# RWKV-7 recurrence in a hybrid decoder step: keys and values on the other head's rows, the values' part taken out of the chunk recurrence, 3 instead of 5 quanta of the next products per late tick

## Chip, cores and metric

One of the eight NeuronCores of a Trainium2 chip runs the kernel. The metric is the device time of one execution in microseconds; the median of several runs counts.

## What is computed

A four-layer decoder trunk (HGRN2, RWKV-7, Mamba-2, HGRN2, each followed by a SwiGLU FFN) is run in fp32 for one prompt of 512 tokens and for 8 sequences of 4 new tokens, with the same weights. Activations lie as 8 tiles of 128 features x 544 tokens (512 prompt, 32 sample). The change concerns the RWKV-7 layer over the prompt. Its recurrence, for each of 16 heads of 64:

```python
def step(s, inp):
    r_t, w_t, k_t, v_t, kk_t, a_t = inp
    sa = jnp.einsum('bhvk,bhk->bhv', s, -kk_t)
    s = (s * w_t[:, :, None, :] + sa[..., None] * (kk_t * a_t)[:, :, None, :]
         + v_t[..., None] * k_t[:, :, None, :])
    return s, jnp.einsum('bhvk,bhk->bhv', s, r_t)
```

After it come a norm by head, a bonus r.k.v, a gate, the output projection and the FFN.

## The kernel before

The prompt's 512 tokens are cut in chunks of 64. A `_Pair` (L998) is two feature tiles, so four heads, over half of the prompt, which is four chunks; there are eight pairs, 0 to 3 for the first half of the tokens and 4 to 7 for the second. The two heads of a tile lie on the row halves 0-63 and 64-127 (`ROWS`, called `e` in the code; `OTH` is the same two, exchanged). A pair is worked off by three generators:

- `front` (L1057) makes for each of its two tiles (`i`) and each chunk (`q`): the transposed values VT, the scores of b and k (BK) against a and r (AR) in one product of 128 columns (masked into SW[0], SB for b and SW[1], SK for k), the transposed b and k (TK), W = SW[1] times VT, the transposed a (AT), and the bonus with `heads_sum` (L973). `keys` (L1015) loads and prepares the operands; its last step writes bn (L1054), of which there are two buffers and which `front` later stores to DRAM (L1121).
- `inv` (L1126) inverts the 64x64 triangular matrices with 32x32 products and ends with U and XA.
- `back` (L1191) walks the four chunks in turn. Per chunk: U += XA z (`psc`, L1206 and L1207), then the state's increment from VT and U (`pp`, L1212), the new state zz (L1215 or L1217), and the output in `po`, which sums VT SK, z R and U SB (L1224). z is scaled on GpSimd first (zd, L1204). At its end O is copied out of PSUM (L1229), the norm by head follows and the gated output is written.

`_rwkv_main` (L874) interleaves them. Stage `s` runs `back` of pair s-2, `inv` of pair s-1 and `front` of pair s, each one step per tick, for twelve ticks. Each tick ends with some quanta of large products: in stages 0 to 5 the r and v projections, in stages 6 to 9 PART = 5 quanta of `end`, the output projection and FFN of the first 256 tokens. A quantum is two of the eight 128-row steps of a product, so six matmuls of 256 columns (`Part.mm`, L265). In this loop TensorE's instructions stand in program order (`ordered`, L73); those of the other engines are placed by the planner. `end` has 298 quanta, of which 240 run in the loop.

After the loop (L666 on) `_Samples` does the recurrence of the 32 sample tokens. At lower priority stand the rest of `end`, then `tail`, the output projection and FFN of the other 288 columns, which needs the samples' output; the last eight steps of `end` come behind `tail`'s first ten.

PSUM tags: `s` (used by `front`) turns over two banks, `m` (`inv`), `c` and `o` (`back`) and `p` (`end`) have their own. Every weight tile of the large products is loaded by SP, rounded by ScalarE (L62) and split by VectorE (L64). An fp32 product shows as two matmul records; lines that all go through `mm` show as L75 and are told apart by their tiles.

Of the kernel before, what the change touches and what calls it, by code (L numbers as in the profile page):

```python
# [12 lines left out]
ALU = mybir.AluOpType  # L13
PSUM = bass.MemoryType.PSUM

P = 128
# [10 lines left out]
class Core:  # L27
# [604 lines left out]
LOW = 4000  # L632
TICKS = 12
PROJ = (24, 6)
PART = 5
ENDS = 78
BANKS = dict(c=1, o=1, p=2)
ROWS = (slice(0, 64), slice(64, 128))
# [3 lines left out]
class Rwkv:  # L642
# [231 lines left out]
    def _rwkv_main(self, layer, st, c, p2):  # L874
# [15 lines left out]
        next(front)  # L890
        quota = 128 - PROJ[0]
        for s in range(10):
            work = [g for g in (pairs[s - 2].back() if s >= 2 else None, inv, front) if g is not None]
            front = inv = None
            for t in range(TICKS):
                for g in work:
                    next(g, None)
                if t == 7 and s < 7:
                    front = pairs[s + 1].front()
                    next(front)  # L900
                n = s * TICKS + t
# [96 lines left out]
class _Pair(_Work):  # L998

    def __init__(self, k, j, st, c, pool, carry):
        self.k, self.j, self.st, self.c, self.pool, self.carry = k, j, st, c, pool, carry
        self.h, self.p = j // 4, j % 4
        self.cols = slice(256 * self.h, 256 * self.h + 256)
# [50 lines left out]
    def front(self):  # L1057

        nc, c, til, psb, mm = self.k.nc, self.c, self.til, self.psb, self.k.mm
        V, ACT, G = nc.vector, nc.scalar, nc.gpsimd  # L1060
        rows = ROWS
# [6 lines left out]
        self.SB, self.SK, self.VT, self.R = (four(n, 3) for n in ("SB", "SK", "VT", "R"))  # L1068
        self.TK = til("TK", [P, 2, 4, 2, 64], 3)
        each = [(q, e) for q in range(4) for e in range(2)]  # L1070
        flat = lambda t: t.rearrange("p a t -> p (a t)")
        mask = lambda a: c["msk"][:, a:a + 64].rearrange("p (o t) -> p o t", o=1).to_broadcast([P, 4, 64])
        for i in range(2):
            AR, BK, v, bn = keys

            ps = psb("s", [P, 4, 64])
            for q, e in each:
                self.turn(ps[rows[e], q], v[rows[e], 64 * q:64 * q + 64], e)
            ACT.copy(out=self.VT[:, i], in_=ps)
            yield  # L1080

            ps = [psb("s", [P, 4, 2, 64]) for _ in range(2)]
            for a in (1, 0):
                for q, e in each:
                    mm(out=flat(ps[a][rows[e], q]), lhsT=BK[rows[e], q, a], rhs=flat(AR[rows[e], q]), start=True, stop=True)
            SW = [til(f"SW{a}", [P, 4, 64]) for a in range(2)]
            for a in (1, 0):
                V.tensor_tensor(out=SW[a], in0=ps[a][:, :, 0], in1=mask(0), op=ALU.mult)
            for a, t in ((1, self.SK), (0, self.SB)):
                V.tensor_tensor(out=t[:, i], in0=ps[a][:, :, 1], in1=mask(64), op=ALU.mult)  # L1090
# [6 lines left out]
            if i == 0:  # L1097
                keys = self.keys(1)
            yield
            ps = psb("s", [P, 4, 2, 64])  # L1100
            for q in range(4):
                for a in range(2):
                    for e in range(2):
                        self.turn(ps[rows[e], q, a], BK[rows[e], q, a], e)
            ACT.copy(out=self.TK[:, i], in_=ps)
            yield
            ps = psb("s", [P, 4, 64])
            for q, e in each:
                mm(out=ps[rows[e], q], lhsT=SW[1][rows[e], q], rhs=self.VT[rows[e], i, q], start=True, stop=True)
            ACT.copy(out=self.W[:, i], in_=ps)  # L1110
            ps = psb("s", [P, 4, 64])
            for q, e in each:
                self.turn(ps[rows[e], q], AR[rows[e], q, 0], e)
            ACT.copy(out=self.AT[:, i], in_=ps)

            dec = self.dec[:, i, 0:4].rearrange("p (c o) -> p c o", o=1).to_broadcast([P, 4, 64])
            G.tensor_tensor(out=self.R[:, i], in0=AR[:, :, 1], in1=dec, op=ALU.mult)
            yield
            ps = self.heads_sum(bn, "s")
            V.tensor_tensor(out=bn, in0=ps, in1=v, op=ALU.mult)  # L1120
            nc.sync.dma_start(out=self.st["b"][2 * self.p + i][:, self.cols], in_=bn)  # L1121
# [69 lines left out]
    def back(self):  # L1191

        nc, h, psb, til, mm = self.k.nc, self.h, self.psb, self.til, self.k.mm
        V, ACT, G = nc.vector, nc.scalar, nc.gpsimd
        TK, U, VT, rows = self.TK, self.U, self.VT, ROWS
        both = [(i, e) for i in range(2) for e in range(2)]
        z = self.carry[:, 2 * self.p:2 * self.p + 2] if h else None
        po = psb("o", [P, 2, 4, 64])
        for q in range(4):
            ch = psb("c", [P, 2, 2, 64])  # L1200
            pu, pp = ch[:, 0], ch[:, 1]
            if z is not None:
                zd = til("zd", [P, 2, 64], 2)
                G.tensor_tensor(out=zd, in0=z, in1=self.dec[:, :, q:q + 1].to_broadcast([P, 2, 64]), op=ALU.mult)  # L1204
                for i, e in both:
                    mm(out=pu[rows[e], i], lhsT=self.XA[rows[e], i, q], rhs=z[rows[e], i], start=True, stop=True)  # L1206
                V.tensor_tensor(out=U[:, :, q], in0=U[:, :, q], in1=pu, op=ALU.add)  # L1207
# [5 lines left out]
            new = til("zz", [P, 2, 64], 3)  # L1213
            if z is None:
                V.tensor_copy(out=new, in_=pp)  # L1215
            else:
                V.tensor_tensor(out=new, in0=zd, in1=pp, op=ALU.add)  # L1217
            for i in range(2):
                terms = [(VT[:, i, q], self.SK[:, i, q]), (U[:, i, q], self.SB[:, i, q])]
                if z is not None:  # L1220
                    terms.insert(1, (z[:, i], self.R[:, i, q]))
                for a, b in terms:
                    for e in range(2):
                        mm(out=po[rows[e], i, q], lhsT=a[rows[e]], rhs=b[rows[e]], start=a is terms[0][0], stop=a is terms[-1][0])  # L1224
# [172 lines left out]
SB = 2  # L1397
# [525 lines left out]
```

## Time and profile before

| | |
|---|---|
| median of 3 runs | 3618.26 us (3615.19 to 3620.75) |
| profiled execution | 3622.13 us, its span 3620.5 us |
| mean granted TensorE clock | 0.961 |
| busy share of the span: PE, DVE, ACT, POOL | 93%, 60%, 38%, 23% |
| RWKV-7 main loop within the span | about 945 to 1536 us |
| samples' part of RWKV-7, until its output projection | to about 1634 us |

PE is TensorE, DVE VectorE, ACT ScalarE, POOL GpSimd. A clock of 1.0 is 2.4 GHz, 0.5 is 1.2 GHz. Busy time of PE counts overlapping records once, so idle time is where no matmul was in flight. In a timeline, a bracket behind a row gives the engine's idle time before it and what released it. In rows of one line's instructions the durations are shortest, median and longest in ns.

### The profile page before, as it was taken

How to read it: one execution, taken by the hardware profiler on the slowest of the kernel's cores; microseconds unless marked ns; L12 is line 12 of the kernel's file. 1: busy time of each engine (PE TensorE's matmuls, PEld its weight loads, DVE VectorE, ACT ScalarE, POOL GpSimd, SP SyncE). 2: the span in 40 equal slices, each digit the busy share in tenths (PEclk: the TensorE clock that was granted, in tenths of full speed). 3: DMA queues.
4: the chain of work that ended last, by engine and by line, in shares of the span. 5: the costliest groups of instructions: out<-in, count | busy, mean ns of one | idle time of the engine just before them, and what ended most of it. 6: DMA issues, size and time to landing. Idle time of an engine off the chain costs nothing.

```text
span 3620.5 us, 83616 instructions
## 1 busy us (share of the span) xinstructions
PE 3365.0 (93%) x35785; PEld 3182.9 (88%) x35785; DVE 2187.0 (60%) x3470; ACT 1384.6 (38%) x2326; POOL 849.8 (23%) x897
## 2 busy tenths in 40 slices
PE   8998999989879799978998889999999999899998
PEld 7887999989768689858998778899999988799998
DVE  6787543465445565656667988664444777754345
ACT  4444322245444454425444333353222534442223
POOL 5554100030223321122003544210000455410001
PEclk9998999999889899989999989999999999899999
DMA  3222322234533333444444434332222322232223
GB/s 122 80 92 87 116 89 90 91 124 161 176 101 114 105 105 126 136 139 143 163 149 121 140 122 149 116 100 88 90 90 86 112 96 85 79 123 88 89 92 108
DMA packets 190818, 405.64 MB, mean 112 GB/s; under 512 B 31712, under 2 KB 94688, under 8 KB 190448
## 3 DMA queue, kind: packets, MB, share of 16 engines
q1 hardware_dynamic: 190448, 400.30, 34.0%
q8 instruction: 282, 4.62, 0.5%
q14 instruction: 88, 0.72, 0.1%
HBM read 355.76 MB, written 43.86 MB: 110 GB/s over the span
## 4 chain that ended last, share of the span: by engine, by line
PE 48%; DVE 8%; DMA 3%; issue 2%; ACT 2%; POOL 1%; SPq 0%; POOLq 0%; DVEq 0%; ACTq 0%
PE big L101 27%; PE psp L75 11%; PE big L91 5%; DVE wlo L64 2%; DMA E<-cumd 1%; DVE E L1585 1%; DVE sq L1529 1%; PE psm L75 1%; ACT whi L62 1%; PE pss L75 1%; DVE sq L1531 0%; DMA out_wkv_s<-s 0%; PE psc L75 0%; DVE ql L502 0%; PE pso L75 0%
## 5 line engine op out<-in xcount | busy, mean ns | idle before, releaser
L62 ACT ACTIVATE whi<-wraw 128x1024 fp32r<-128x1024 f32 (+2 forms) x585 | 597.5, 1023 | 1388.2 <-issue 750.6
L64 DVE TENSOR_TENSOR wlo<-wraw,whi 128x1024 fp32r<-128x1024 f32 (+2 forms) x585 | 715.1, 1223 | 207.4 <-ACT whi L62 202.6
L101 PE MATMUL big<-nl,whi 128*128 128x256 f32 (+1 forms) x3600 | 766.6, 292 | 0.0
L101 PE MATMUL big<-nh,wlo 128*128 128x256 f32 (+1 forms) x3600 | 758.5, 291 | 2.4 <-DVE wlo L64 2.4
L101 PE MATMUL big<-nh,whi 128*128 128x256 f32 (+1 forms) x3600 | 754.5, 289 | 2.2 <-DVE fr L439 1.2
L101 PEld LDWEIGHTS big<-nh,whi 128*128 128x128 f32 x3600 | 585.3, 190 | 12.0 <-issue 8.4
L101 PEld LDWEIGHTS big<-nl,whi 128*128 128x128 f32 x3600 | 584.5, 190 | 7.8 <-issue 6.2
L101 PEld LDWEIGHTS big<-nh,wlo 128*128 128x128 f32 x3600 | 579.5, 190 | 10.7 <-issue 5.8
L138 POOL TENSOR_TENSOR acc<-acc,sq 128x256 f32<-128x256 f32 (+1 forms) x126 | 120.5, 956 | 1612.5 <-ACT sq L137 1611.2
L75 PE MATMUL psp<-nh,whi 128*128 128x256 f32 (+1 forms) x848 | 265.0, 312 | 10.3 <-ACT nh L68 8.6
L75 PE MATMUL psp<-nh,wlo 128*128 128x256 f32 (+1 forms) x848 | 249.8, 295 | 14.4 <-DVE wlo L64 14.4
L75 PE MATMUL psp<-nl,whi 128*128 128x256 f32 (+1 forms) x848 | 249.5, 294 | 0.7 <-DVE nl L69 0.7
L220 DVE TENSOR_TENSOR fg<-fg,big 128x544 f32<-128x544 f32 x66 | 47.6, 721 | 234.9 <-PE big L101 232.4
L75 PEld LDWEIGHTS psp<-nh,whi 128*128 128x128 f32 x848 | 168.0, 198 | 24.4 <-ACT nh L68 10.1
L75 PEld LDWEIGHTS psp<-nh,wlo 128*128 128x128 f32 x848 | 168.7, 199 | 18.2 <-DVE wlo L64 16.3
L75 PEld LDWEIGHTS psp<-nl,whi 128*128 128x128 f32 x848 | 168.2, 198 | 2.3 <-DVE nl L69 1.2
L216 DVE TENSOR_TENSOR fg<-big,rs 128x544 f32<-128x544 f32 x66 | 47.8, 724 | 199.3 <-PE big L101 188.5
L229 DVE TENSOR_TENSOR fd<-big,rs 128x544 f32<-128x544 f32 (+2 forms) x96 | 55.5, 581 | 177.8 <-PE big L101 159.5
L101 PE MATMUL big<-hh,wlo 128*128 128x256 f32 (+1 forms) x768 | 158.8, 288 | 0.0
L101 PE MATMUL big<-hh,whi 128*128 128x256 f32 (+1 forms) x768 | 158.0, 287 | 0.0
L101 PE MATMUL big<-hl,whi 128*128 128x256 f32 (+1 forms) x768 | 157.9, 287 | 0.0
L75 PE MATMUL psp<-x,whi 128*128 128x288 f32 x704 | 141.0, 295 | 0.0
(611 smaller groups left out, 6965.3 us busy)
## 6 DMA issues: line engine op xcount, KB each, us to landing
wraw<-in_ffn_gate SPq DMA_DIRECT2D x110, 512.0 KB, 3.2
wraw<-in_ffn_up SPq DMA_DIRECT2D x110, 512.0 KB, 3.2
wraw<-in_ffn_down SPq DMA_DIRECT2D x80, 512.0 KB, 3.5
wraw<-in_hg_in SPq DMA_DIRECT2D x64, 512.0 KB, 3.3
wraw<-in_ffn_down SPq DMA_DIRECT2D x64, 384.0 KB, 3.1
wraw<-in_rw_in SPq DMA_DIRECT2D x40, 512.0 KB, 3.9
wraw<-in_mb_in SPq DMA_DIRECT2D x40, 512.0 KB, 3.3
wraw<-in_hg_out SPq DMA_DIRECT2D x32, 512.0 KB, 3.2
```

Source lines behind the costliest of these rows:

```text
L62: nc.scalar.activation(out=hi, in_=raw, func=AF.Copy)
L64: nc.vector.tensor_tensor(out=lo, in0=raw, in1=hi.bitcast(F32), op=ALU.subtract)
L75: i = self.nc.tensor.matmul(**kw)
L91: self.nc.tensor.matmul(out=ps[0:cols, HALF[h]], lhsT=a[:, k, c0:c0 + cols], rhs=b[:, HALF[h]], start=first, stop=last)
L101: self.nc.tensor.matmul(out=ps[0:cols, HALF[h]], lhsT=a[:, k, c0:c0 + cols], rhs=b[:, HALF[h]], start=first, stop=last)
L138: (eng or nc.gpsimd).tensor_tensor(out=acc, in0=acc, in1=sq, op=ALU.add)
L216: V.tensor_tensor(out=g, in0=pg, in1=rs, op=ALU.mult)
L220: V.tensor_tensor(out=g, in0=g, in1=pu, op=ALU.mult)
L229: V.tensor_tensor(out=d[:, c], in0=ps[:, c], in1=rs[:, c], op=ALU.mult)
L1529: V.scalar_tensor_tensor(out=acc[:, s:512], in0=raw[:, 0:512 - s], scalar=cw, in1=acc[:, s:512], op0=ALU.mult, op1=ALU.add)
L1585: V.tensor_scalar(out=E[:, h], in0=E[:, h], scalar1=tok[:, 1, c, g * 8 + h:g * 8 + h + 1], scalar2=0.0, op0=ALU.subtract, op1=ALU.min)
```

## The change

- The transposed values VT and the transposed k (now KT) are written to the rows of the other head, and so are the masked scores with k (SW[1], and SR for the former SK). For that, the products with k write to the other row half and to a second PSUM bank, and the products of b and k for the two heads are issued in turn, four on four different quadrants of the array. The turns of b and k, and W with the turns of a, are issued in the same way.
- The state's increment from the values (PV = KT VT) and the values' part of the output (OV = VT SR) are computed in `front` for all chunks, in its last step ahead of `heads_sum`, and copied to SBUF by ScalarE. `back` keeps only the U and z terms: PV is added to zd on GpSimd (or used as zd in the first chunk), OV is added when O leaves PSUM, now on VectorE instead of a copy on ScalarE.
- PART goes from 5 to 3.
- In a tick `inv` now goes ahead of `back`.

```diff
-PART = 5
+PART = 3
-            work = [g for g in (pairs[s - 2].back() if s >= 2 else None, inv, front) if g is not None]
+            work = [g for g in (inv, pairs[s - 2].back() if s >= 2 else None, front) if g is not None]
...
+            VT, KT, SR = (til(n, [P, 4, 64], d) for n, d in (("VT", 2), ("KT", 1), ("SR", 1)))
             ps = psb("s", [P, 4, 64])
             for q, e in each:
-                self.turn(ps[rows[e], q], v[rows[e], 64 * q:64 * q + 64], e)
-            ACT.copy(out=self.VT[:, i], in_=ps)
+                self.turn(ps[oth[e], q], v[rows[e], 64 * q:64 * q + 64], e)
+            ACT.copy(out=VT, in_=ps)
...
-            for a in (1, 0):
-                for q, e in each:
-                    mm(out=flat(ps[a][rows[e], q]), lhsT=BK[rows[e], q, a], rhs=flat(AR[rows[e], q]), start=True, stop=True)
+            place = (rows, oth)
+            for q, e in each:
+                for a in range(2):
+                    mm(out=flat(ps[a][place[a][e], q]), lhsT=BK[rows[e], q, a], rhs=flat(AR[rows[e], q]), start=True, stop=True)
...
-            ps = psb("s", [P, 4, 2, 64])
+            ps = [psb("s", [P, 4, 64]) for _ in range(2)]
+            for q, e in each:
+                for a in range(2):
+                    self.turn(ps[a][place[a][e], q], BK[rows[e], q, a], e)
+            ACT.copy(out=self.TB[:, i], in_=ps[0])
+            ACT.copy(out=KT, in_=ps[1])
+            yield
+            ps = [psb("s", [P, 4, 64]) for _ in range(2)]
             for q in range(4):
-                for a in range(2):
-                    for e in range(2):
-                        self.turn(ps[rows[e], q, a], BK[rows[e], q, a], e)
-            ACT.copy(out=self.TK[:, i], in_=ps)
...
+                for e in range(2):
+                    mm(out=ps[0][rows[e], q], lhsT=SW[1][oth[e], q], rhs=VT[oth[e], q], start=True, stop=True)
+                for e in range(2):
+                    self.turn(ps[1][rows[e], q], AR[rows[e], q, 0], e)
+            ACT.copy(out=self.W[:, i], in_=ps[0])
+            ACT.copy(out=self.AT[:, i], in_=ps[1])
...
+            for t, x, y in ((self.PV, KT, VT), (self.OV, VT, SR)):
+                ps = psb("s", [P, 4, 64])
+                for q, e in each:
+                    mm(out=ps[rows[e], q], lhsT=x[oth[e], q], rhs=y[oth[e], q], start=True, stop=True)
+                ACT.copy(out=t[:, i], in_=ps)
             ps = self.heads_sum(bn, "s")
...
+            zd = self.PV[:, :, q]
             if z is not None:
                 zd = til("zd", [P, 2, 64], 2)
                 G.tensor_tensor(out=zd, in0=z, in1=self.dec[:, :, q:q + 1].to_broadcast([P, 2, 64]), op=ALU.mult)
+                G.tensor_tensor(out=zd, in0=zd, in1=self.PV[:, :, q], op=ALU.add)
...
+            for i, e in both:
+                mm(out=pp[rows[e], i], lhsT=self.TB[rows[e], i, q], rhs=U[rows[e], i, q], start=True, stop=True)
+            new = til("zz", [P, 2, 64], 3)
+            V.tensor_tensor(out=new, in0=zd, in1=pp, op=ALU.add)
             for i in range(2):
-                for x, a, first in ((VT, 1, True), (U, 0, False)):
+                if z is not None:
                     for e in range(2):
-                        mm(out=pp[rows[e], i], lhsT=TK[rows[e], i, q, a], rhs=x[rows[e], i, q], start=first, stop=not first)
...
+                        mm(out=po[rows[e], i, q], lhsT=z[rows[e], i], rhs=self.R[rows[e], i, q], start=True, stop=False)
+                for e in range(2):
+                    mm(out=po[rows[e], i, q], lhsT=U[rows[e], i, q], rhs=self.SB[rows[e], i, q], start=z is None, stop=True)
...
-        ACT.copy(out=O, in_=po.rearrange("p i c t -> p (i c t)"))
+        V.tensor_tensor(out=O, in0=po.rearrange("p i c t -> p (i c t)"), in1=self.OV.rearrange("p i c t -> p (i c t)"), op=ALU.add)
```

## Rows read from the trace of the kernel before

**Rows 1.** Windows by stage: stretch, length, busy us by engine, PEclk, DMA share, GB/s.

```profile
1200.00:1259.00 59.00, 49.63 (x1176) 43.07 (x1174) 29.04 (x58) 26.44 (x57) 17.81 (x27) 0.91 0.31 96
...
1343.00:1417.00 74.00, 71.25 (x1406) 66.20 (x1403) 44.66 (x80) 34.24 (x62) 13.52 (x15) 1.00 0.36 115
1417.00:1483.00 66.00, 63.72 (x1202) 59.14 (x1201) 40.66 (x67) 31.27 (x48) 7.74 (x8) 1.00 0.37 127
...
1520.00:1580.00 60.00, 53.03 (x456) 46.64 (x455) 41.79 (x68) 24.35 (x35) 12.11 (x18) 0.91 0.54 162
1580.00:1640.00 60.00, 32.85 (x261) 19.65 (x260) 28.32 (x47) 9.95 (x18) 21.77 (x28) 0.69 0.37 113
```

**Rows 2.** Chain of waits, late stages: start us, us, engine, tile, line, records.

```profile
1266.22 1.89 PE pss L75 x32
...
1272.93 1.08 PE pss L75 x32
...
1279.76 1.08 PE pss L75 x32
...
1392.40 0.86 PE psu L75 x2
...
1434.38 0.70 PE pso L75 x24
1435.76 3.76 PE psp L75 x30
```

**Rows 3.** Timeline of PE, one tick of stage 8: start us, us, instruction, records.

```profile
1433.86 0.28 PE L75 MATMUL psc<-U,TK 64*64 64x64 f32 x4
1433.98 0.28 PE L75 MATMUL psc<-VT,TK 64*64 64x64 f32 x4
...
1435.01 0.75 PE L75 MATMUL psm<-X,Y 32*32 32x32 f32 x64
1435.69 0.38 PE L75 MATMUL psp<-nh,whi 128*128 128x256 f32 x1
```

**Rows 4.** Timeline of PE, products of 512 columns on parts of the array.

```profile
1571.19 1.08 PE L1348 MATMUL pss<-s,AR 64*64 64x512 f32 x4
...
2012.57 1.07 PE L1690 MATMUL pse<-E,C 128*32 128x512 f32 x8
```

**Rows 5.** Timelines of DVE and PE in stage 8: a state and a U, made and used.

```profile
1435.33 0.28 DVE L1217 TENSOR_TENSOR zz<-zd,psc 128x128 f32<-128x128 f32 x1
1440.76 0.28 DVE L1207 TENSOR_TENSOR U<-U,psc 128x128 f32<-128x128 f32 x1
...
1439.45 0.45 PE L75 MATMUL psc<-zz,XA 64*64 64x64 f32 x8
...
1444.44 0.28 PE L75 MATMUL psc<-U,TK 64*64 64x64 f32 x4
```

**Rows 6.** Timelines of DVE and PE in stage 4, around tick 6.

```profile
1162.20 0.48 DVE L1054 SCALAR_TENSOR_TENSOR bn<-lr,rvec,la 128x256 f32<-128x256 f32 x1 [4.93 <-DMA db<-bn]
1162.60 0.28 DVE L1217 TENSOR_TENSOR zz<-zd,psc 128x128 f32<-128x128 f32 x1
...
1162.93 0.45 PE L75 MATMUL psc<-zz,XA 64*64 64x64 f32 x8 [1.68 <-DVE zz L1217]
```

**Rows 7.** Instructions of four lines: line, engine, count, durations ns, first and last start.

```profile
L1079 ACT COPY VT<-pss x16: 356/372/377, 946.7 to 1381.1; 128x256 f32<-128x256 f32 x16
...
L1229 ACT COPY O<-pso x8: 567/586/587, 1068.3 to 1517.1; 128x512 f32<-128x512 f32 x8
...
L1188 DVE TENSOR_TENSOR XA<-psm,dec x8: 673/678/684, 1026.1 to 1482.2; 128x512 f32<-128x512 f32 x8
...
L1204 POOL TENSOR_TENSOR zd<-zz,dec x24: 401/402/1428, 1033.5 to 1507.6; 128x128 f32<-128x128 f32 x24
```

**Rows 8.** Waits of PE in stage 0; timeline of ACT in stage 4.

```profile
PE pss L75 <- ACT W L1110: 2.0, 1, 2.0
...
1146.05 1.22 ACT L1094 COPY NN<-SW 32x128 f32<-32x128 f32 x4 [3.80 <-DVE SW L1088]
```

**Rows 9.** Waits in 1522 to 1660 us: in total us, times, longest us.

```profile
PEld psp L75 <- ACT a L68: 12.6, 1, 12.6
```

More of the change, by code (lines that the diff above doesn't have):

```diff
@@ L1060, in front @@
         V, ACT, G = nc.vector, nc.scalar, nc.gpsimd
-        rows = ROWS
+        rows, oth = ROWS, OTH
         four = lambda tag, bufs: til(tag, [P, 2, 4, 64], bufs)
@@ L1067, in front @@
         self.W, self.AT = four("W", 2), four("AT", 2)
-        self.SB, self.SK, self.VT, self.R = (four(n, 3) for n in ("SB", "SK", "VT", "R"))
-        self.TK = til("TK", [P, 2, 4, 2, 64], 3)
+        self.SB, self.TB, self.PV, self.OV, self.R = (four(n, 3) for n in ("SB", "TB", "PV", "OV", "R"))
         each = [(q, e) for q in range(4) for e in range(2)]
@@ L1074, in front @@
             AR, BK, v, bn = keys
+            VT, KT, SR = (til(n, [P, 4, 64], d) for n, d in (("VT", 2), ("KT", 1), ("SR", 1)))
             ps = psb("s", [P, 4, 64])
             for q, e in each:
-                self.turn(ps[rows[e], q], v[rows[e], 64 * q:64 * q + 64], e)
-            ACT.copy(out=self.VT[:, i], in_=ps)
+                self.turn(ps[oth[e], q], v[rows[e], 64 * q:64 * q + 64], e)
+            ACT.copy(out=VT, in_=ps)
             yield
             ps = [psb("s", [P, 4, 2, 64]) for _ in range(2)]
-            for a in (1, 0):
-                for q, e in each:
-                    mm(out=flat(ps[a][rows[e], q]), lhsT=BK[rows[e], q, a], rhs=flat(AR[rows[e], q]), start=True, stop=True)
+            place = (rows, oth)
+            for q, e in each:
+                for a in range(2):
+                    mm(out=flat(ps[a][place[a][e], q]), lhsT=BK[rows[e], q, a], rhs=flat(AR[rows[e], q]), start=True, stop=True)
             SW = [til(f"SW{a}", [P, 4, 64]) for a in range(2)]
-            for a in (1, 0):
+            for a in range(2):
                 V.tensor_tensor(out=SW[a], in0=ps[a][:, :, 0], in1=mask(0), op=ALU.mult)
-            for a, t in ((1, self.SK), (0, self.SB)):
-                V.tensor_tensor(out=t[:, i], in0=ps[a][:, :, 1], in1=mask(64), op=ALU.mult)
+            for a, t in ((1, SR), (0, self.SB[:, i])):
+                V.tensor_tensor(out=t, in0=ps[a][:, :, 1], in1=mask(64), op=ALU.mult)
             for e in range(2):
@@ L1099, in front @@
             yield
-            ps = psb("s", [P, 4, 2, 64])
-            for q in range(4):
-                for a in range(2):
-                    for e in range(2):
-                        self.turn(ps[rows[e], q, a], BK[rows[e], q, a], e)
-            ACT.copy(out=self.TK[:, i], in_=ps)
[L1106 to L1114, printed above, removed]
+            ps = [psb("s", [P, 4, 64]) for _ in range(2)]
+            for q, e in each:
+                for a in range(2):
+                    self.turn(ps[a][place[a][e], q], BK[rows[e], q, a], e)
[3 more added lines that the diff above has]
+            ps = [psb("s", [P, 4, 64]) for _ in range(2)]
+            for q in range(4):
+                for e in range(2):
[4 more added lines that the diff above has]
+            ACT.copy(out=self.AT[:, i], in_=ps[1])
             dec = self.dec[:, i, 0:4].rearrange("p (c o) -> p c o", o=1).to_broadcast([P, 4, 64])
@@ L1194, in back @@
         V, ACT, G = nc.vector, nc.scalar, nc.gpsimd
-        TK, U, VT, rows = self.TK, self.U, self.VT, ROWS
+        U, rows = self.U, ROWS
         both = [(i, e) for i in range(2) for e in range(2)]
@@ L1208, in back @@
             yield
+            for i, e in both:
+                mm(out=pp[rows[e], i], lhsT=self.TB[rows[e], i, q], rhs=U[rows[e], i, q], start=True, stop=True)
+            new = til("zz", [P, 2, 64], 3)
+            V.tensor_tensor(out=new, in0=zd, in1=pp, op=ALU.add)
             for i in range(2):
-                for x, a, first in ((VT, 1, True), (U, 0, False)):
+                if z is not None:
                     for e in range(2):
-                        mm(out=pp[rows[e], i], lhsT=TK[rows[e], i, q, a], rhs=x[rows[e], i, q], start=first, stop=not first)
[L1213 to L1224, printed above, removed]
+                        mm(out=po[rows[e], i, q], lhsT=z[rows[e], i], rhs=self.R[rows[e], i, q], start=True, stop=False)
+                for e in range(2):
+                    mm(out=po[rows[e], i, q], lhsT=U[rows[e], i, q], rhs=self.SB[rows[e], i, q], start=z is None, stop=True)
             z = new
```

## Prediction, made before the changed kernel was run

> **What bounds the kernel now.** I read the windows by stage first, because the change touches only the RWKV-7 main loop (ten stages `s` of twelve ticks `t`) and what runs after it. Stage starts are the VT copies of tick 0. In the early stages TensorE is not full: stage 5 takes 59 us with 49.6 busy, 9.4 us idle. In the late stages it nearly is: stage 7 has 71.25 of 74 us and stage 8 63.72 of 66. After the loop it starves: 7.0 us idle in 1520 to 1580 and 27.2 us in 1580 to 1640, the latter at a mean granted clock of 0.69, so part of it at 1.2 instead of 2.4 GHz [rows 1]. The chain of waits, which reaches back to 1256 us, names the content of a late tick: five quanta of the first half's output projection and FFN, 30 matmuls in 3.76 us, and beside them short groups of square products, 0.70 us for the output terms of one chunk [rows 2]. So a late tick is paid in TensorE time, an early stage partly in waits, and the stretch after the loop in waits for the decode samples' serial work.
>
> **Four square products at a time.** Today the scores of one tile are 16 products of 128 columns in 1.89 us, the 16 turns of keys 1.08 us, and W with the turns of A 1.08 us [rows 2]. Each product leaves two records, and the two heads' products already run as a pair. The question is whether four quadrants run together where two did. Rows of 512 columns show the halves of it: one full-array product takes 0.86 us [rows 2]; two products on different row halves take 1.08 us together, and four on different column strips 1.07 us [rows 4]. So either direction packs almost freely; both together stand in no row. If four take the time of two, the scores fall by about 0.9 us and the other two groups by 0.5 us each. For the 64-column groups the pace of records can stand in the way: 32 products of 32 columns need 0.68 us to the next group (64 records, 10.6 ns each) [rows 3]. If a record of twice the width costs twice that, four products need 0.17 us where two pairs now need 0.236 (0.118 each), so the gain is 0.3 instead of 0.5 us a group. Per tile the saving is 1.5 to 1.9 us; with 16 tiles 24 to 30 us, and zero if quadrants don't overlap. I take 25, near the packed rows.
> The Trainium skill, page TensorEngine Tiling (Array Packing), Restrictions and Gotchas, says that different row tiles can't access the same PSUM bank simultaneously; by that rule the four would run one after the other and the 25 us be zero. The trace disagrees as far as it goes: the two row halves of L1348 write one bank and take 1.08 us, not twice 0.86 [rows 4].
>
> **Values out of the recurrence.** Each chunk of `back` loses its VT terms: two pairs for the state and two for the output, at 0.118 us a pair [rows 3], so 0.47 us a chunk, 1.9 us for two tiles. PV and OV bring the same 16 pairs per two tiles into `front`; their row and column halves are all crossed, so only two quadrants work and they save nothing. TensorE's sum is zero. What moves is the place: `front`'s last step gets 0.94 us of products ahead of `heads_sum`, and `back`'s ticks get shorter. In early stages `back` is often not what TensorE is short of: at tick 6 of stage 4 it waited 1.68 us for zz, because DVE stood 4.93 us at the bn write for the store of an earlier bn [rows 6]. That store follows `heads_sum`, so shaving the tick between only lengthens this wait. I give back 5 us of the early stages' savings for that (0.47 us, at two such ticks in each of stages 2 to 5, and a little for stages 0 and 1); bounds 0 and 15.
>
> **More evacuations.** Per tile ACT copies TB and KT (0.37 us each) where TK took one copy as wide as O's, 0.59 us, and PV and OV (0.37 each) on top: about 0.9 us, 14 us in all. O's copy of 0.59 us leaves ACT, and DVE adds OV at about the 0.68 us of the equally wide XA [rows 7]. ACT and DVE aren't full in these stages (26.4 and 29.0 of 59 us in stage 5) [rows 1], so throughput costs nothing; latency may. Three uses of two banks now fall in one step: PV, OV, then `heads_sum` in PV's bank. TensorE stands in order, so `heads_sum`, the projections and everything behind it wait for ACT's copy of PV. With ACT free that is a copy of 0.37 us against 0.47 us of OV products: near nothing. With ACT busy it is what `heads_sum` once waited for W's copy, 2.0 us [rows 8]. Most such steps show no wait today, so I take 0.5 us, 8 us over 16 tiles; bounds 0 and 32. POOL gets 28 more additions of 0.40 us [rows 7] on zd; from zz to its next use lie two ticks, so I cost them at nothing; without that cover it is 0.4 us times 28, 11 us. O on DVE instead of ACT: 2 us, for eight head norms that wait a little behind the masks; bounds -1 and 5. The order inverse, then `back`, changes neither cycle's length: I take zero, bounds -4 and 4.
>
> **Fewer products per late tick.** PART from 5 to 3 takes 2 quanta, 12 matmuls, out of 48 ticks: 2/5 of 3.76 less the switch of about 0.2 us gives 1.43 us, so 68.5 us leave the loop. Whether the ticks really shrink depends on slack. In stage 8, zz was ready at 1435.61 and used at 1439.45; U ready at 1441.04 and used at 1444.44 [rows 5]: 3.8 and 3.4 us of slack, against 1.43 taken. The short-tick stage 5 has 9.4 us idle, the late stages 2.3 to 2.8 [rows 1]; four times the difference, some 28 us, is the upper bound of new waits, 0 the lower. By the slack I take 6.
> The 96 quanta aren't gone. They run after the loop beside the samples. There 34 us were idle in 120. Where such work was at hand (1520 to 1580), idle was 12%; at that rate 120 us hold 106 us of products instead of 86 [rows 1]. So 20 us of the 68.5 vanish in holes and 48.5 come back behind. With fewer holes the clock should stay up too: the 32.85 us busy at 0.69 would be 10 us shorter at full clock, of which I take 4. Bounds: nothing at all (the samples stretched on DVE and ACT by the extra weight splits) and 44 us (all idle and all of that clock).
>
> **Sum**, against the profiled execution of 3622.1 us (span 3620.5): packing -25, given back +5, PV wait +8, O on DVE +2, late waits +6, holes -20, clock -4: -28 us, so 3594. The median of the runs is 3618.3, 4 us below that execution, so I forecast **3590 us**.
>
> **Rivals.** First, *the four products don't overlap*. Against it stand [rows 4]; for it, that no row has both directions. Then -25 goes, and the +5 with it: -8, so 3610. Second, *the holes aren't filled*: the samples' work is stretched by as much as the products fill, since each quantum of four brings a weight split on ACT and DVE, and the samples' output projection still waits for ACT a (12.6 us at once) [rows 9]. Then -24 goes: -4, so 3614. Third, on the other side, *the wait for PV's copy takes the place*. Place: ticks 4 and 10 of stages 0 to 7. ACT is in order, and if PV's copy falls behind a copy that itself waits, such as NN, which idled ACT 3.80 us for DVE [rows 8], TensorE stops 16 times. At 3.8 us instead of 0.5 that is +53, so +25 and 3643. It decides from about 2.7 us a time (28 + 7 over 16, on top of 0.5); the 2.0 us row is just below.
> The Trainium skill, page TensorEngine Tiling (Array Packing), Performance Considerations, says that tiling speeds up TensorE but not PSUM evacuation, and that after it the copy may become the bottleneck; that is this third case, and stage 5's ACT at 26.4 of 59 us [rows 1] speaks against it as a matter of throughput.
>
> **How the numbers follow.** My forecast has a chance of 0.55, no overlap 0.13, holes not filled 0.17, the PV wait 0.15. Good ends together (packing 30, holes and clock 44, no new waits but 6) would give -68, 3550; I cut that end at 3558, and the upper one at 3625, beyond no change, leaving most of the third case out. A measurement of this kernel can tell about 0.2%, 7 us, from no change. Faster by more: nearly all of the forecast and about half of the first two rivals, which lie at that limit, 0.70. Within it: 0.15. Slower: the third rival, 0.15.
>
> **What would show it.** Right: score groups near 1 us and turns near 0.6 in stages 6 and 7; 18 matmuls in about 2.3 us per late tick and stages 7 and 8 some 17 us shorter; idle under 20 us in the 120 after the loop; the loop ending some 75 to 80 us earlier. Wrong: unchanged 1.89 and 1.08 us (first rival); PE idle after the loop still above 30 us or a samples' chain longer by 25 (second); PE pss waiting for ACT PV with microseconds a time (third); late stages with 8 or more us idle, which would say that the slack rows misled me.

## The result, and the profile after

The changed kernel takes 3572.94 us (median of four runs, 3567.18 to 3580.03) beside 3618.86 us for the kernel before in the same measurement: a ratio of 0.9875, 95% interval 0.9854 to 0.9897, so 46 us faster. A second measurement (e5) gave 0.9854 (0.9832 to 0.9875). Its profiled execution took 3576.0 us (span 3574.3), 46 us under that of before.

These are the windows of the profile: stretch, its length, busy us of PE, PEld, DVE, ACT and POOL with record counts, granted TensorE clock, DMA share, GB/s. First stages 0 to 5 of the kernel before, a stretch that the rows ahead of the prediction don't show:

```profile
945.00:1256.00 311.00, 258.63 (x6000) 226.54 (x6000) 159.38 (x304) 139.75 (x304) 97.08 (x143) 0.91 0.37 113
```

Then the changed kernel: stages 0 to 5, stages 6 to 9, and what lies between the loop and the first product of the samples' output projection.

```profile
946.00:1266.00 320.00, 248.50 (x6112) 212.78 (x6111) 165.25 (x314) 148.09 (x343) 104.97 (x157) 0.87 0.37 114
1266.00:1456.00 190.00, 176.51 (x3791) 160.17 (x3779) 122.80 (x219) 94.52 (x178) 54.26 (x72) 0.96 0.33 108
1456.00:1600.00 144.00, 134.57 (x1196) 115.92 (x1195) 112.67 (x174) 59.91 (x87) 38.47 (x46) 0.99 0.59 187
```

The three stretches tell three stories. In the **early stages** TensorE has 10.1 us less to do (258.63 to 248.50) and the stages still became 9 us longer: it idles 71.5 us instead of 52.4, and the clock fell with it. In the **late stages** 79 us are gone. **After the loop** TensorE is now full: 9.4 us idle of 144 at a clock of 0.99, where the rows of before had 27.2 us idle in 60 at 0.69 [rows 1].

The next table is worked out from the timeline of TensorE in each profile: early is from the first turn of v in stage 0 to that of stage 6, late from there to the second head sum of the last pair's head norm, after from there to the first product of the samples' output projection. Ratios stand to the kernel before in the same measurement; 0.001 is 3.6 us. Two profiles of the changed kernel differ by 3 us in the early stages, so differences of that size say nothing.

| kernel | ratio (95%) | early | late | after |
|---|---|---|---|---|
| before | 1 | 310.3 | 269.3 | 109.8 |
| changed | 0.9875 (0.9854-0.9897) | 319.3 | 190.0 | 144.1 |
| changed, again | 0.9854 (0.9832-0.9875) | 316.1 | 190.1 | 146.5 |
| e1 before, PART 3 | 0.9920 (0.9900-0.9940) | 313.6 | 204.6 | 148.0 |
| e2 changed, PART 5 | 0.9948 (0.9929-0.9967) | 322.4 | 254.4 | 107.7 |
| e3 PV and OV in one bank | 0.9901 (0.9880-0.9922) | 333.0 | 190.7 | 146.7 |
| e4 fours as pairs | 0.9889 (0.9869-0.9909) | 319.9 | 195.2 | 145.0 |
| e6 old order | 0.9890 (0.9872-0.9908) | 312.4 | 201.4 | 148.6 |
| e7 four bn | 0.9877 (0.9856-0.9899) | 314.9 | 190.7 | 145.4 |
| e8 four bn, one bank | 0.9838 (0.9819-0.9857) | 311.5 | 194.0 | 143.8 |
| e9 before, PART 3, new order | 0.9947 (0.9935-0.9960) | 319.8 | 200.6 | 149.4 |
| e10 changed, PART 2 | 0.9938 (0.9924-0.9951) | 321.4 | 176.0 | 182.0 |
| e11 values one tick later | 0.9864 (0.9850-0.9877) | 322.2 | 188.9 | 147.6 |
| e12 that and four bn | 0.9821 (0.9803-0.9839) | 304.2 | 188.4 | 147.2 |

Of the profiled 46 us, 70.3 leave the loop, 34.3 come back after it, 2.6 leave the rest of RWKV-7, and some 8 lie in layers that the change doesn't touch; such parts differ by up to 12 us between profiles, and no reason is read from them.

**The fours do run together.** The timeline of TensorE in stage 6 of the changed kernel: start us, us, instruction, records.

```profile
1295.57 0.32 PE L75 MATMUL pss<-AR,BK 64*64 64x128 f32 x1
...
1295.68 1.04 PE L75 MATMUL pss<-AR,BK 64*64 64x128 f32 x30
1296.65 0.39 PE L75 MATMUL psp<-nh,whi 128*128 128x256 f32 x1
...
1298.98 0.69 PE L75 MATMUL psm<-TI,N 32*32 32x32 f32 x32
...
1300.66 0.69 PE L75 MATMUL pss<-ident,BK 64*64 64x64 f32 x32
1301.28 0.39 PE L75 MATMUL psp<-nh,whi 128*128 128x256 f32 x1
...
1305.30 0.27 PE L75 MATMUL pss<-VT,SW 64*64 64x64 f32 x2
...
1305.92 0.39 PE L75 MATMUL psp<-nh,whi 128*128 128x256 f32 x1
```

From its first score to the next group the scores take 1.08 us (chain row of before: 1.89), the turns of keys 0.62 (1.08), W with the turns of A 0.62 (1.08) [rows 2]; the 18 matmuls of three quanta take 2.33 us (1296.65 to 1298.98).

**The late copy of PV.** The longest entries among TensorE's waits in 946 to 1266 us of the changed kernel, each with us in total, times and longest; then the first rows of the view of line 1126's copies that say who waited for them, over the whole loop:

```profile
PE pss L75 <- ACT PV L1126: 29.1, 9, 7.7
PE psu L75 <- ACT fs L984: 9.3, 3, 3.6
PE psm L75 <- DVE TI L1166: 6.4, 5, 3.5
...
PE psm L75 <- DVE XA L1196: 4.0, 3, 2.2
```

```profile
its engine sat idle before it (us, times) until:
  PE pss L75: 1.4, 3
who waited for it (us, times):
  PEld pss L75: 38.9, 13
  PE pss L75: 37.0, 12
```

ACT sat idle for PV's products only 1.4 us in all, while TensorE waited 37.0 us in 12 of 16 places for a copy of 0.37 us. So the copy stood in ACT's queue behind other work. The longest but one of these waits, in stage 2, on three engines:

```profile
1084.10 0.51 PE L75 MATMUL pss<-VT,KT 64*64 64x64 f32 x11
...
1092.62 1.22 PE L75 MATMUL pss<-bn,blk 128*128 128x256 f32 x2 [7.54 <-ACT PV L1126]
...
1086.54 0.42 ACT L1032 ACTIVATE eg<-gc 128x256 f32<-128x256 f32 x1 [2.96 <-DVE AR L1053]
...
1087.13 1.06 ACT L62 ACTIVATE whi<-wraw 128x1024 fp32r<-128x1024 f32 x1
1088.42 0.60 ACT L1048 ACTIVATE la<-la,oka,rvec 128x256 f32<-128x256 f32 x1 [0.23 <-POOL b L1046]
1088.93 0.57 ACT L1191 COPY U<-psm 128x512 f32<-128x512 f32 x1
1091.22 1.09 ACT L1252 ACTIVATE O<-O,rvec 128x256 f32<-128x256 f32 x2 [1.73 <-DVE O L994]
1092.22 0.35 ACT L1126 COPY PV<-pss 128x256 f32<-128x256 f32 x1
...
1089.98 1.21 DVE L994 TENSOR_TENSOR O<-O,fv 128x512 f32<-128x512 f32 x1 [0.51 <-POOL fv L992]
```

PV's products (VT,KT) were done by 1084.61. Ahead of its copy ACT did eg for the next keys, which waited 2.96 us for DVE's AR, then a weight split, la, U, and O of a head norm, which waited 1.73 us for DVE. TensorE stood all that time at `heads_sum` with everything behind it. The longest wait, in stage 5, has the same row of operations ahead of it. In five other places it was la of the next keys, which waited 2.5 to 3.3 us for POOL's b, and in four more the exponential of a head norm with the reload of its function table (last section), which waited for nobody.

### The profile page after: what moved, and what is told of

It reads as the page before. It is cut to its first block, busy times and chain, and to the rows that moved or that the text cites. A ratio compares the mean times of both kernels' runs of the same rounds, so it can differ in the third digit from the quotient of the medians.

```text
span 3574.3 us, 83682 instructions
## 1 busy us (share of the span) xinstructions
PE 3331.1 (93%) x35785; PEld 3147.9 (88%) x35785; DVE 2200.1 (62%) x3478; ACT 1388.7 (39%) x2364; POOL 865.7 (24%) x925
## 5 line engine op out<-in xcount | busy, mean ns | idle before, releaser
L101 PEld LDWEIGHTS big<-nh,wlo 128*128 128x128 f32 x3600 | 579.1, 190 | 13.3 <-issue 8.7
```

The costliest lines, as they stand in the source:

```text
L101: self.nc.tensor.matmul(out=ps[0:cols, HALF[h]], lhsT=a[:, k, c0:c0 + cols], rhs=b[:, HALF[h]], start=first, stop=last)
```

## The experiments

**e1, the filling alone.** The kernel before with one edit.

```diff
-PART = 5
+PART = 3
```

> The kernel before with PART 3 instead of 5 and nothing else. Theory (the holes): the gain of the change is the 96 quanta that fill TensorE's idle time beside the samples; in the two traces the loop's last stages became 76 us shorter, of which 68 are moved products, and only 32 us came back after the loop. Then PART alone gives nearly the whole gain: 30 to 38 us less than before, about 3585, with under 15 us of TensorE idle between the loop's end and the samples' output projection. Rival (the packing): the products moved come back in full behind the loop and the gain is the four-quadrant packing; then this run is within 7 us of before, 3611 to 3625.

Measured 3600.06 us, 0.992: 29 us by the ratio, just under the 30 to 38 expected. The late stages fell by 64.7 us and 38.2 came back after the loop, where 11.5 us of TensorE are idle. So the filling alone is more than half of the change's gain, and holes are filled.

**e2, all but the filling.** The reverse edit in the changed kernel.

> The changed kernel with PART back at 5. Theory (the holes): most of the gain goes, 3600 to 3612, since the packing's 28 us of TensorE time are largely eaten by the wait of heads_sum for the copy of PV (37 us in the changed kernel's trace). The late stages are then about 68 us longer again and the idle time after the loop is back near 31 us in 98. Rival (the packing): it stays at 3573 to 3585.

Measured 3608.72 us, 0.9948: 19 us under before. The two parts add up: 29 and 19 are 48, the whole is 45 to 53 by its two ratios. The stretch after the loop in this kernel has again its holes and its low clock:

```profile
1524.00:1632.00 108.00, 77.09 (x657) 56.22 (x657) 63.62 (x102) 30.07 (x45) 31.94 (x43) 0.80 0.46 137
```

From this row to 1456:1600 above, 539 records of TensorE are added, which is 90 of the 96 quanta at six records each (the quanta of the last three ticks stand behind the mark in both kernels). They bring 57.5 us of busy time (77.09 to 134.57), 21.5 us of holes close (30.91 to 9.43), and the stretch grows by 36.

**e3, PV and OV in one bank** with one copy, so that `heads_sum` takes the other bank.

```diff
-            for t, x, y in ((self.PV, KT, VT), (self.OV, VT, SR)):
-                ps = psb("s", [P, 4, 64])
+            ps = psb("s", [P, 2, 4, 64])
+            for b, x, y in ((0, KT, VT), (1, VT, SR)):
                 for q, e in each:
-                    mm(out=ps[rows[e], q], ...
-                ACT.copy(out=t[:, i], in_=ps)
+                    mm(out=ps[rows[e], b, q], ...
+            ACT.copy(out=self.PO[:, :, i], in_=ps)
```

> The changed kernel with PV and OV in one PSUM bank, one tile and one copy, so that heads_sum takes the other bank and no longer stands behind the copy made in the same tick. Theory: the wait of heads_sum for PV cost time of its own, 37 us in 12 waits; about half of it is gained, since part of it hid waits that come next (the bn store, the head norm's square): 3548 to 3562, and heads_sum waits under 8 us in all. Rival: the late copy only shows that ScalarE is late; what it does next is needed as urgently, so the same time is waited for elsewhere: 3567 to 3578.

Measured 3591.72 us, 0.9901: 9 to 17 us above the changed kernel by its two ratios (only the interval of the first overlaps), not faster. The theory fell, and the rival's range was missed too. No wait for PV is left, and these stand in 946 to 1279 us of this kernel, TensorE's first and then DVE's longest:

```profile
PE psm L75 <- DVE XA L1198: 16.4, 5, 5.0
PE psm L75 <- ACT U L1193: 11.8, 4, 3.7
PE psm L75 <- DVE TI L1168: 10.4, 5, 3.9
...
DVE bn L1055 <- DMA db<-bn: 31.5, 9, 6.1
```

`heads_sum` is no longer late, and DVE now stands 31.5 us (23.0 in 9 in the changed kernel) at the bn write, for the store of an earlier bn, with XA and TI behind it. It is the wait of [rows 6].

**e4, the fours issued as pairs.** The same products and places, but all of one operand's pairs ahead of the other's.

```diff
-            for q, e in each:
-                for a in range(2):
+            for a in range(2):
+                for q, e in each:
                     mm(out=flat(ps[a][place[a][e], q]), ...
```

(and in the same way for the turns of BK, and W ahead of the turns of A)

> The changed kernel with the products that now follow four by four issued two by two: all of one row placement, then all of the other; same products, same banks, same copies. Theory: the packing works (scores of a stage 3.79 before, 2.02 us after) and saves 28 us of TensorE time over 16 tiles, but in the early stages half of it is eaten by waits: 12 to 18 us slower than the changed kernel, 3585 to 3591, the scores back near 1.89 us a tile. Rival a: all of it counts, 3598 to 3604. Rival b: none counts, TensorE waits for something else in every stage: 3568 to 3578.

Measured 3586.13 us, 0.9889. That is 5 to 13 us above the changed kernel by its two ratios, whose intervals overlap with this one. The time is as expected, but the scores are not back near 1.89 us. These are the scores in stage 6 of this kernel, of the same tile as in the timeline above, and what follows them:

```profile
1294.27 1.54 PE L75 MATMUL pss<-AR,BK 64*64 64x128 f32 x32
1295.74 0.39 PE L75 MATMUL psp<-nh,whi 128*128 128x256 f32 x1
```

They take 1.47 us to the next group, and this tile's turns of keys and W with the turns of A take 0.90 each. So the pairs still overlap in part, and the run undoes 0.95 us a tile of the 1.73 that the fours save: little more than half of the packing. In the profile the late stages lose 5 us and the early ones nothing (319.9 against 319.3 and 316.1), though TensorE is busy 2.4 us longer there than in the changed kernel (248.50):

```profile
945.00:1265.00 320.00, 250.93 (x6115) 217.94 (x6114) 160.75 (x308) 146.75 (x340) 101.61 (x156) 0.90 0.37 111
```

So what this half of the packing saves is seen as time only where TensorE is full; no run leaves out the whole of it.

**The changed kernel again** (e5), as a base for the next three on their chip.

> The changed kernel once more, beside the three that follow, so that they are compared on one chip. Every theory expects its ratio to the kernel before at 0.985 to 0.990, and stage times in the loop within some 8 us of the first profile, since parts of the program that no change touches (the first 945 us, the Mamba-2 layer, the last HGRN2 layer) differed by up to 12 us from run to run.

Measured 3573.91 us, 0.9854.

**e6, the old order**, `back` ahead of the inverse.

```diff
-            work = [g for g in (inv, pairs[s - 2].back() if s >= 2 else None, front) if g is not None]
+            work = [g for g in (pairs[s - 2].back() if s >= 2 else None, inv, front) if g is not None]
```

> The changed kernel with back ahead of inv in each tick again. Theory: the order changes no cycle's length; within 7 us of the changed kernel on the same chip. Rival: with inv first, the inverse's products, which the prediction costed at nothing, are ready earlier and part of the gain is the order's; then this run is 8 to 15 us slower than the changed kernel, with XA and TI waits growing.

Measured 3586.86 us, 0.989: 13 us slower than the changed kernel in the same measurement. So the order, which the prediction had at zero, counts here. It is the late stages (201.4 against 190.0):

```profile
1255.50:1457.00 201.50, 183.48 (x3771) 164.72 (x3770) 121.64 (x222) 95.50 (x180) 59.05 (x73) 0.95 0.34 107
```

Of the 11.5 us more, 7.0 are busy time and 4.5 idle; no single wait carries them, and the waits for XA and TI that the rival named don't grow there. The timelines show where the busy time comes from. In the new order the products of `back` stand right ahead of those of `front`, and the two run together; in the old order the inverse stands between them. A tick of stage 7 with W in it, first in the changed kernel, then in e6:

```profile
1341.28 0.22 PE L75 MATMUL pso<-SB,U 64*64 64x64 f32 x1
1341.28 0.22 PE L75 MATMUL pss<-VT,SW 64*64 64x64 f32 x1
...
1334.96 0.28 PE L75 MATMUL pso<-SB,U 64*64 64x64 f32 x4
1335.17 0.75 PE L75 MATMUL psm<-X,Y 32*32 32x32 f32 x64
1335.86 0.27 PE L75 MATMUL pss<-VT,SW 64*64 64x64 f32 x2
```

Worked out from the timelines, a product of `back` or `front` (tiles psc, pso, pss) was in flight for 38.0 us of the late stages in the changed kernel and for 44.4 us in e6: 6.4 of the 7.0 us. The early stages were 4 to 7 us shorter here.

**e7, four buffers of bn.**

```diff
-        bn = til("bn", [P, 256], 2)
+        bn = til("bn", [P, 256], 4)
```

> The changed kernel with four buffers for bn instead of two, nothing else. Theory: in the early stages time is set by waits in VectorE's order; it stood 23 us in 9 waits for the store of an earlier bn, and zz, TI and XA are queued behind. Without that wait the early stages get 10 to 20 us shorter. Rival: another wait takes its place (the wait of heads_sum for PV, 29 us in 9, stays): within 7 us of the changed kernel.

Measured 3579.31 us, 0.9877: no difference from the changed kernel that can be told. DVE no longer waits for the store at the bn write but 13.3 us for la on POOL (944 to 1259 us), and TensorE's wait for PV stays:

```profile
DVE bn L1055 <- POOL la L1049: 13.3, 9, 2.3
...
PE pss L75 <- ACT PV L1126: 28.8, 9, 8.1
```

**e8, both cures**: e3 and e7 together.

> Both at once: four buffers for bn, and PV and OV in one bank with one copy, so that neither heads_sum waits for PV nor VectorE for the bn store. With one bank alone the 29 us of waits for PV in the early stages came back as waits for XA, U, TI and Y, and VectorE's wait for the bn store rose from 23 to 31.5 us. Theory (the waits are links of one chain, and the bn store is the next link): 15 to 30 us faster than the changed kernel. Rival (the early stages are bound by the engines' orders as a whole): within 7 us of it.

Measured 3570.06 us, 0.9838. That lies 4 us under the changed kernel by the medians on the same chip, inside its interval, as the rival had it. But beside e3 (0.9901) the same four buffers are worth 23 us, where they are worth nothing beside the changed kernel. This called for e11 and e12.

**e9, the order and the filling alone.** The kernel before with PART 3 and e6's line in its new form.

> The kernel before with two edits of the change alone: three quanta of filling a late tick instead of five, and the inverse ahead of the back half in each tick. The square products stay as they were. With three quanta alone this kernel was 0.992 of the kernel before. Theory, the order is worth its 11 to 13 us wherever the late ticks are short: 0.988 to 0.989, about 3587 to 3590 us, and the stages 6 to 9 together 8 us or more shorter than with three quanta alone (204.6 us there). Rival, the order pays only with the fours and with the values out of the recurrence: 0.991 to 0.993, about 3597 to 3602 us, and the late stages within 3 us of 204.6.

Measured 3605.87 us, 0.9947, above e1's 0.992 with overlapping intervals, and above the ranges of theory and rival. The theory fell: without the fours and the values the order gains nothing. The late stages are 4.0 us shorter than e1's and the early ones 6.2 longer. In the changed kernel the sign was the same (late 11 shorter, early 4 to 7 longer), and only there the first outweighs the second. Part of why the late stages gain more there is the overlap of `back` and `front`: it is worth 3.4 us here (52.2 in e1 to 48.8) and 6.4 there. The rest, and the longer early stages, stay open, and so does the mixed order, old in stages 0 to 5 and new after, which wasn't tried.

**e10, two quanta.**

```diff
-PART = 3
+PART = 2
```

> The changed kernel with two quanta in a late tick instead of three: 48 quanta more, some 34 us of products by the 0.72 us of one, leave the loop. Theory, three is already past the best: the stretch after the loop has only 9 us idle left, so what leaves the loop comes back behind it in full, and the shorter ticks cannot shrink by all they lose because the inverse and the back half then wait for their copies: 3575 to 3595 us, the stretch after the loop 30 us or more longer than 146. Rival, the late ticks still hide waits that fewer quanta expose nowhere and the decode samples overlap further: 3555 to 3568 us.

Measured 3601.56 us, 0.9938: 23 to 30 us slower than three by its two ratios, and above the 3575 to 3595 expected. Windows of this kernel: from the start of stage 7 to the head norm in stage 8, then the stretch after the loop.

```profile
1320.00:1412.00 92.00, 77.31 (x1990) 67.97 (x1978) 42.60 (x90) 40.02 (x81) 20.15 (x30) 0.91 0.24 76
...
1442.00:1624.00 182.00, 168.43 (x1465) 149.07 (x1464) 135.63 (x207) 72.56 (x102) 40.40 (x46) 0.98 0.57 180
```

After the loop the quanta that moved between the marks, 45 of the 48, come back whole: 33.9 us more busy time than in 1456:1600 above, and 4 us more idle. In the loop TensorE idles 14.7 us of 92 in the first window, at a clock of 0.91, and this stretch is no shorter than with three quanta (89 us from 1328.4 to 1417.6 in the changed kernel). TensorE no longer sets its length; that the chains of inverse and `back` do is the likely reading, though no one wait carries it.

**e11, the values one tick later.** `heads_sum` keeps its tick, and PV and OV take the next one, which was empty.

```diff
-            for t, x, y in ((self.PV, KT, VT), (self.OV, VT, SR)):
-                ...
             ps = self.heads_sum(bn, "s")
             V.tensor_tensor(out=bn, in0=ps, in1=v, op=ALU.mult)
             nc.sync.dma_start(out=self.st["b"][2 * self.p + i][:, self.cols], in_=bn)
+            yield
+            for t, x, y in ((self.PV, KT, VT), (self.OV, VT, SR)):
+                ...
             if i == 0:
                 yield
-            yield
```

> The changed kernel with the head sum first at its tick and the PV and OV products with their copies one tick later, where the front half had nothing to do; so no head sum stands behind the copy of PV. Theory, the place of PV's copy is what costs the early stages: of the 37 us that TensorE waited for it two thirds go, the stages 0 to 5 are 290 to 305 us together instead of 319, and the time is 3550 to 3562 us. Rival, the early stages are bound by the orders of ACT and DVE as a whole: the wait turns up at other copies (XA, U, TI, Y), stages 0 to 5 stay within 8 us of 316, and the time is 3566 to 3582 us.

Measured 3575.46 us, 0.9864: the same as the changed kernel, so the rival held. The 29.1 us are gone, and in 946 to 1268 us there stand instead, TensorE's and then DVE's:

```profile
PE psm L75 <- ACT U L1191: 13.3, 4, 4.0
...
PE psm L75 <- DVE XA L1196: 7.8, 3, 4.5
...
DVE bn L1055 <- DMA db<-bn: 34.5, 12, 4.9
```

**e12, the values later and four buffers of bn.**

> The changed kernel with both cures of its two longest waits in the early stages: PV and OV one tick later, as in the run before (0.9864), and four buffers of bn instead of two. With one bank for PV and OV the same four buffers were worth 0.0063 of the kernel before (0.9901 to 0.9838), some 22 us. Theory, the two waits hide each other, so that a cure pays only beside the other: DVE's wait for the store of bn, 33 us in 11 there, goes, stages 0 to 5 come under 312 us from 322, and the ratio is 0.979 to 0.983, about 3550 to 3562 us. Rival, what is left is the orders of the engines as a whole: the waits go over to la, U and XA, stages 0 to 5 stay within 8 us of 320, the ratio is 0.984 to 0.988.

Measured 3562.76 us, 0.9821 (0.9803 to 0.9839): 16 us under e11, 12 to 20 under the changed kernel by its two ratios (its interval overlaps a little with that of the second), 65 under the kernel before; the lowest ratio of all, though its interval overlaps with e8's. The theory held, with 304.2 us in the early stages. The windows of stages 0 to 5, and DVE's wait at the bn write in 949 to 1253 us:

```profile
948.00:1253.00 305.00, 243.93 (x6114) 210.57 (x6113) 165.26 (x311) 148.41 (x341) 103.89 (x157) 0.89 0.40 118
```

```profile
DVE bn L1055 <- POOL la L1049: 14.1, 9, 2.3
```

So with PV in the way (changed kernel and e7) four buffers are worth nothing, and with PV out of the way (e3 to e8, e11 to e12) 23 and 16 us, which the early stages show as well (333.0 to 311.5, 322.2 to 304.2); with two buffers PV's removal is worth nothing or less, with four 14 and 20 us in its two forms (0.9877 to 0.9838 and 0.9821). Two waits covered each other, and either cure alone shows nothing.

## Why the prediction was right, and where its sum was not

The forecast was 3590 us, the result 3573: inside the range, faster, by 46 us where 28 were forecast. The runs split these into 29 for the filling (e1) and 19 for the rest (e2). The prediction's terms for the filling, +6, -20 and -4, make 18; its other terms, -25, +5, +8 and +2, make 10. Both halves were too small. That the second is not further off is luck: its errors offset each other, since the packing was counted in stages where no gain shows, and the order, put at zero, was worth 13 us.

**The filling: the late waits and the clock were mis-sized.** Of the 68.5 us, 64.4 lie ahead of the mark at which the late stages end (45 ticks at 1.43 us), and from e2 to the changed kernel these stages shrink by 64.4 us (254.4 to 190.0). So the term for late waits, +6, was about zero, and the slack of [rows 5] was to be taken at its word; stages 7 and 8, from the first product with the carried state in stage 7 to that in stage 9, fell by 34.6 us together (134.8 to 100.2) where twice 17 was asked. Of the bound of 28 us nothing came; e10 shows where it begins, one quantum lower. The holes were right, 21.5 us measured for 20. The clock was worth more than put down: the 64.4 us of products appear as 57.5 us of added busy time behind the loop, while the mean granted clock of that stretch rose from 0.80 to 0.99. That is 6.9 us, where 4 were taken out of the 10 that the row of 0.69 gave [rows 1]; what products that merely overlap have in it is not separated. The two, with no late waits, make 28.4 us, and e1 measured 29. The second rival (holes not filled) is dead: 34 to 38 us came back, not 64, and the samples' work, from its first instruction to its last, took 98.9 us instead of 94.1, not 25 more. It now ends 28 us ahead of the samples' output projection (1571.9 to 1600.3 us), and TensorE runs the rest of `end` meanwhile.

**The packing: the instructions right, the worth too high.** The three groups fell to 1.08, 0.62 and 0.62 us; the prediction asked for 1 and 0.6. Per tile that is 0.81 + 0.46 + 0.46 = 1.7 us, inside its 1.5 to 1.9. The first rival (no overlap) is dead, and the records' pace made no limit. The Trainium skill, page TensorEngine Tiling (Array Packing), Restrictions and Gotchas, says that different row tiles can't access one PSUM bank simultaneously; in the fours both row halves write each of the two banks, and the runs disagree with it for these products. In the kernel before, the pairs already wrote one bank from both row halves, so the prediction's step from that rule to a gain of zero did not follow. The failed step is that 25 us were counted as time in all stages. Of the 16 tiles 12 lie in the early stages, and these aren't bound by TensorE's work: busy time fell there by 10.1 us, and the time rose; even with both long waits cured (e12) they are only 6 us shorter than before (304.2 against 310.3), where 12 tiles at 1.73 us make 21. e4 prices little more than half of the packing at 5 to 13 us, and the part of it that its profile shows within the loop lies in the late stages. What the whole packing is worth in time, no run shows. The prediction read stage 5 as paid partly in waits [rows 1] and then subtracted from it all the same, except for the +5.

**The wait for PV's copy: the rival's mechanism, at some 60% of its price.** It was costed at 0.5 us a time, 8 us, and by the rival at 3.8 us, 61 us; measured are 37.0 us in 12 of 16 places, 3.1 us each time, but 2.3 us over all 16, under the 2.7 us from which the third rival was to decide. The failed step is the choice of 0.5 because "most such steps show no wait today": today's copy, W's, stands in another tick and so at another place in ACT's queue. What falls just ahead of PV's copy is the next keys' eg and la and the head norm's work, and these wait for DVE and POOL or reload a function table. That ACT was busy only 26.4 of 59 us [rows 1] said nothing on it: in the changed kernel the queue, not the load, made it late. The Trainium skill, the same page, Performance Considerations, says that the copy out of PSUM may become the bottleneck after a fourfold speedup of TensorE; the trace agrees that TensorE came to wait for it, but by its place in the order and not by throughput. Even so the time fell, because most of this wait stands in for others that would have come: removing it alone brought nothing (e11) or a loss (e3). A wait's length in the profile was not its worth.

**Giving back 5 us at the bn write** was the right wait at the right place. In the changed kernel it holds DVE 23.0 us in 9 and was itself hidden behind PV's; e12 shows what the two are worth together, 12 to 20 us.

**The order at zero** was wrong by more than its bounds of -4 and 4: 13 us in this kernel (e6), none in the kernel before with short ticks (e9). The working "changes neither cycle's length" left out that the products of a tick stand in one line on TensorE, and that neighbours in it can overlap: `back` beside `front` gives 6.4 of the 11.4 us in the late stages. What gives the rest, mostly idle time, isn't shown.

**The end of the loop** came 68.8 us earlier (1525.0 to 1456.2 us), not 75 to 80: the early stages' 9 us.

**O on DVE and the additions on POOL** have no run of their own. DVE never waited for zd on POOL in the loop of the changed kernel, so the nothing put down for those additions stands; the 2 us for O weren't measured.

## What to carry to other kernels

Fewer products in the ticks of a chain pay as long as the slack rows say so and a starving stretch lies behind to take the rest; once that stretch is full (9 us idle of 144), every further quantum moved comes back whole. A saving on an engine counts, as far as these runs show, only in the stages where that engine is full, so multiply it by those stages alone. Where two long waits stand in one stretch, cure both in one run before either is judged worthless: here each alone gave nothing and both gave 12 to 20 us.

## What the runs showed of the hardware that was not expected

Four products on the four 64x64 quarters of the array ran together nearly as if one pair stood alone, with two PSUM banks written at once: 16 products of 128 columns in 1.08 us instead of 1.89, of 64 columns in 0.62 instead of 1.08. The order of issue matters: with one operand's pairs ahead of the other's (e4) the same products took 1.47 and 0.90 us.

ACT reloads a function table twice in each head norm, 1.28 us each time. In the changed kernel, ahead of the stage 2 wait shown above:

```profile
1079.05 1.28 ACT L987 ACT_TABLE_LOAD   x1
1080.34 0.63 ACT L987 ACTIVATE fs<-fv 128x512 f32<-128x512 f32 x1
1080.99 1.28 ACT L988 ACT_TABLE_LOAD   x1
1082.28 0.63 ACT L988 ACTIVATE fs<-fs 128x512 f32<-128x512 f32 x1
1082.93 0.37 ACT L1115 COPY W<-pss 128x256 f32<-128x256 f32 x1
```

The two loads take more of ACT's queue than the logarithm and the exponential that they serve (2.56 against 1.26 us), and copies of PSUM stand behind them.

A stop of TensorE was paid twice here. The windows of its 7.54 us wait in stage 2 and of what followed:

```profile
1084.90:1092.60 7.70, 0.18 (x7) 0.04 (x2) 5.27 (x6) 4.10 (x9) 5.61 (x7) 0.80 0.34 119
1092.60:1096.00 3.40, 3.38 (x24) 2.95 (x26) 1.09 (x3) 0.24 (x1) 1.05 (x1) 0.50 0.32 86
```

Behind the wait TensorE ran 3.4 us at 0.50, 1.2 GHz, so by an estimate half of that, 1.7 us, is to be added to the stop.
